# A hybrid decoder layer on one core: the second up projection with wide products, and its weight sums made in DRAM by GpSimd

## The chip, the core and the metric

The kernel runs on one core of one Trainium2 chip. The metric is the device time of one execution in microseconds (us); the median of three executions stands for a kernel. A core has five engines with one instruction queue each, worked off in order: PE (TensorE, matrix products, with PEld for loading the stationary operand), DVE (VectorE), ACT (ScalarE), POOL (GpSimd) and SP (SyncE, which here only issues transfers). Transfers run on 16 DMA engines that all issuing engines share.

## The reference

One layer of a decoder over 512 tokens of width 1024, in float32:

```python
x = x + 0.5 * swiglu(rmsnorm(x, ffn1_norm), ffn1_wg, ffn1_wu, ffn1_wd)
x = x + hybrid_mixer(rmsnorm(x, mix_norm), w_in, ...)     # attention and recurrence, 64 small products
x = x + 0.5 * swiglu(rmsnorm(x, ffn2_norm), ffn2_wg, ffn2_wu, ffn2_wd)
out = rmsnorm(x, final_norm)

def swiglu(x, w_gate, w_up, w_down):                      # 1024 -> 2816 -> 1024
    return (silu(x @ w_gate) * (x @ w_up)) @ w_down
```

## The kernel before

**Precision.** The products take a rounded float32 type. A weight tile `wr` is split by `wsplit` into a rounded part `wh` (a copy on ACT) and the remainder `wl` (a subtraction on DVE), and an activation likewise into two parts, so a float32 product becomes three matmuls: high by high, high by remainder and remainder by high.

**Stages, in order of time.** First up projection (a direct part, then a block part), first down projection, the mixer (`run_jobs`, 64 jobs named by `ORDER`; most have 24 matmuls of 512 columns, the eight `A` jobs have 12), second up projection, second down projection. Both up projections are the function `ffn_up`, both down projections `block_down`.

**`ffn_up`.** Eight direct products come first (`direct`). The other weights are taken in 2 by 2 blocks, with seven block products in place of eight: 18 groups `w` in the second up projection, and so 126 products in the list `stream`, each named by a number `p` from 1 to 7 and a group. A product has four k-steps of 128. Its moving operands (`moving_operands`) are tiles `cm` whose left 256 columns (`lo`) are the rounded part and whose right 256 (`hi`) the remainder. The seven products need sums of weight blocks, s1 to s4. `load` brings the blocks of a group into SBUF (SP), adds two of them to others in flight (transfers by POOL with an addition), and `add_weights` makes the last two sums on DVE. `prepare` splits the weights of the product four ahead (`LEAD`). `results` takes a finished product out of PSUM: ACT copies, DVE adds or multiplies, ACT applies silu.

**The mixer's order.** `run_jobs` is written out by a planner: `Plan` keeps a clock for each engine, and `due` issues the next step of a chain when the plan says that its inputs are there. `mixer_begin` (at the second k-step of a job) copies the high part of the weights of the job two later, `mixer_prepare` (at the fourth) makes the remainder. `gate_weights` loads the small gate weights `wrg` of the eight recurrent jobs x0 to x7, three jobs ahead (`AHEAD`), by POOL into a tile `gr`, which ACT then copies to `gw`. Between the jobs the weight sums of the second down projection are made in DRAM (`Blocks`, `sums_in_turn`): the first two transfers of a block by SP, the other six by POOL; of a kernel's 64 such transfers 16 stand in SP's queue and 48 in POOL's.

**Buffers.** Raw weights `wr` have three buffers (`RAWS`), the split parts `wh` and `wl` three each, a PSUM tag (`mm`, `aux`) four banks each.

Of the kernel before, what the change touches and what calls it, by code (L numbers as in the profile page):

```python
# [9 lines left out]
F32 = mybir.dt.float32  # L10
# [33 lines left out]
LEAD = 4  # L44
PLAIN, PAIRS, TAIL = 6, 8, 3
DIRECT = 4
SUMJOBS = 48


ORDER = """  # L50
# [125 lines left out]
def hybrid_kernel(ctx, tc, xt, vec, w1u, w1d, wm, wki, wrg, watt, wrnn, wout, w2u, w2d, gf, out):  # L176
# [139 lines left out]
    class Blocks:  # L316
# [6 lines left out]
        def stages(self):  # L323
            plain, adds = nc.gpsimd.dma_start, lambda o, i: nc.gpsimd.dma_start(o, i, accum_op=ALU.add)  # L324
            return [
                [(nc.sync.dma_start, self.s1, self.a21), (nc.sync.dma_start, self.s3, self.a21)],
                [(adds, self.s1, self.a22), (adds, self.s3, self.a11)],
                [(plain, self.s2, self.s1)],
                [(adds, self.s2, self.a11)],
                [(plain, self.s4, self.s2)],  # L330
                [(adds, self.s4, self.a12)],
            ]

    def sums_in_turn(blocks):

        lists, groups = [b.stages() for b in blocks], []
        for n in range(len(lists) + 5):
            groups.append([t for u in range(max(0, n - 5), min(n + 1, len(lists))) for t in lists[u][n - u]])
        return groups

    def moving_operands(g):

# [56 lines left out]
        V.tensor_mul(tu, tu, tg)  # L399
        return tu  # L400

    def ffn_up(y, wu, n0, hs, g, waiting=(), given=(), ahead=None):

# [6 lines left out]
        H = KD // 2 * P  # L410
        f0 = n0 + DIRECT
        count = KF - f0
        ws = []

        direct = [(n, j) for n in range(n0, f0) for j in range(2)]
        raws, split_, sums, gates = list(given), [], [], []

        def fetch():
            if len(raws) < len(direct):
                r = raw.tile([P, WMAX], F32, tag="raw", name=nm("wr"))  # L420
                Q.dma_start(r, wu[direct[len(raws)]])
                raws.append(r)

        def prepare_direct():
# [30 lines left out]
        class W:  # L455
            pass

        def load(w):

# [31 lines left out]
                V.tensor_add(o.s4, o.s2, o.x[:, H:])  # L491

        def prepare(i):
            if i < LEAD:
                add_weights(i)
            if i + 1 >= LEAD:
                add_weights(i + 1)
            p, w = stream[i]
            o = ws[w]
            if i % 2 == 0:  # L500
                units.append([wsp.tile([P, WMAX], F32R, tag=t, name=nm(t)) for t in ("wh", "wl")])
            h, l = (t[:, i % 2 * H:(i % 2 + 1) * H] for t in units[i // 2])
            wsplit({1: lambda: o.x[:, :H], 2: lambda: o.x[:, H:], 6: lambda: o.s2, 5: lambda: o.s1, 7: lambda: o.s3,
                    4: lambda: o.a22, 3: lambda: o.s4}[p](), h, l)

        def products(i):
            p, w = stream[i]
            o = ws[w]
            if p == 1:
                o.beta = psum("mm")  # L510
            elif p == 2:
                o.p2 = psum("aux")
            elif p == 5:
                o.gamma = psum("aux")
            acc_ = {2: lambda: o.p2, 5: lambda: o.gamma, 3: lambda: o.gamma}.get(p, lambda: o.beta)()[:, lo]
            h, l = (t[:, i % 2 * H:(i % 2 + 1) * H] for t in units[i // 2])
            starts, opens = p in (1, 2, 5), dict(skip_group_check=p not in (1, 2, 5))
            for j in range(KD // 2):
                c = slice(j * P, (j + 1) * P)
                m = moving[{1: "n11", 2: "b21", 6: "t2", 5: "t1", 7: "r", 4: "q", 3: "n22"}[p]][j]  # L520
                T.matmul(acc_, h[:, c], m[:, lo], start=starts and j == 0, stop=False, **opens)
                T.matmul(acc_, h[:, c], m[:, hi], start=False, stop=False, **opens)
                T.matmul(acc_, l[:, c], m[:, lo], start=False, stop=j == KD // 2 - 1, **opens)

        def results(i):
            p, w = stream[i]
# [30 lines left out]
        with tc.manual_schedule(engines=ENGINES):  # L557
# [4 lines left out]
            for d, (n, j) in enumerate(direct):  # L562
# [13 lines left out]
                if d == 0:  # L576
                    for _ in range(3):
                        next(norm)
                if d in (4, 6):
                    load_ = load(len(ws))  # L580
                if d >= 4:
                    next(load_, None)
                if d > 1:
                    next(operands, None)
# [4 lines left out]
                pass  # L589
            for i in range(len(stream)):  # L590
                products(i)
                if i:
                    results(i - 1)
                else:
                    together(results_direct(len(direct) - 1))
                if i + LEAD < len(stream):
                    prepare(i + LEAD)
                elif not ahead or i + LEAD - len(stream) < PLAIN - f0:
                    halve(hs, f0 + i + LEAD - len(stream))
                if ahead:  # L600
                    ahead(i - len(stream))
                if i % 14 == 12 and i // 14 < f0:
                    halve(hs, i // 14)
                if i % 7 == 1 and len(ws) < count:
                    load_ = load(len(ws))
                next(load_, None)
            results(len(stream) - 1)

    def halve(hs, n):

# [252 lines left out]
    d1 = block_down(hs, w1d, sums)  # L863
    ffn_up(y, w1u, 2, hs, V_G1, ((WP[0], WP[1]), (WP[2], pu)), AH[1:], d1.tasks_at)

    BLOCKS2D = down_blocks(w2d)
    cc = const.tile([P, 8], F32, name="cc")
    hb = vt[:, V_BX:V_BX + 8]

# [401 lines left out]

    idles = []
    lasts, starts_ = {}, {}
    sum_groups, sums_done = sums_in_turn(BLOCKS2D), [0]

    def run_jobs():
        ws = mixer_ws
# [2 lines left out]
        for i, job in enumerate(jobs):  # L1280
# [6 lines left out]
            for k in range(n):  # L1287
# [10 lines left out]
                if k == 2:  # L1298
                    due_sums = len(sum_groups) * (i + 1) // SUMJOBS
                    while sums_done[0] < min(due_sums, len(sum_groups)):  # L1300
                        for move, o, s_ in sum_groups[sums_done[0]]:
                            move(o, s_)
                        sums_done[0] += 1
                if k == 3:
                    mixer_prepare()
                    mixer_fetch()
                if k == n - 1:
# [456 lines left out]
        then(lastD + m - 1, norm_second, m, 1)  # L1764
        then(lastD + m + 1, scaled, m)

    ffn_up(y2, w2u, 0, hs, V_G2, ahead=tasks_at)
# [88 lines left out]
```

## Time and profile before

| what | value |
|---|---|
| median of three executions | 1070.22 us (1070.16 to 1070.58) |
| the profiled execution | 1070.87 us, span 1068.9 us |
| first up projection, block part (78 to 238 us) | PE busy 160.00 of 160 us, DVE 122.38, ACT 92.40 |
| mixer (350 to 728 us) | PE busy 377.63 of 378 us, DVE 314.00, ACT 251.88, POOL 37.80 |
| second up projection, block part (768.5 to 950 us) | PE busy 181.50 of 181.5 us, DVE 137.66, ACT 103.84, POOL 29.83 |
| second down projection (950 us to the end) | PE busy 112.01 of 118.9 us, DVE 88.69, ACT 67.80 |

The span runs from the first to the last instruction of the profiled execution; some 2 us lie around it. Busy shares are of a stage's time. Nearly every instruction has line L170, a helper that records all operations for the planner, so the groups are told apart by the names of their tiles: `wl<-wr,wh` is the remainder of a raw weight, `mm<-cm,wh` a product of a moving operand with a high part.

### The profile page before, as it was taken

What the parts mean: (1) busy time and instruction counts of PE and PEld (TensorE: products, weight loads), DVE (VectorE), ACT (ScalarE), POOL (GpSimd) and SP (SyncE); (2) the same over time, 40 slices, a digit from 0 to 9 for tenths busy, and PEclk for the clock granted to TensorE, in tenths of its full rate; (3) what the DMA queues carried; (4) which work ended last, traced back from release to release, by engine and by line L of the source; (5) the groups of instructions that cost most, each with busy time, mean ns of one, the idle gap of its engine ahead of it and who ended that gap; (6) DMA issues with size and microseconds to landing.
All of it is one profiled execution on the core that took longest, in us unless ns stands there. A gap on an engine that the chain in (4) does not pass through costs nothing.

```text
span 1068.9 us, 17652 instructions
## 1 busy us (share of the span) xinstructions
PE 1058.7 (99%) x6412; PEld 947.6 (89%) x6412; DVE 847.3 (79%) x1614; ACT 658.6 (62%) x1279; POOL 168.2 (16%) x210
## 2 busy tenths in 40 slices
PE   9999999999999999999999999999999999999997
PEld 7889999999989888888888888888899999998886
DVE  6687777779979779999899867766877777779865
ACT  6565655556466657976886664446656555565663
POOL 0161111102341011212120000001511111100020
PEclk9999999999999999999999999999999999999999
DMA  7297767638994486676593211434977776635583
GB/s 277 70 256 192 171 181 203 158 107 238 236 236 118 120 235 165 178 194 181 121 223 107 79 50 50 138 105 112 250 193 165 185 195 170 158 101 175 178 207 128
DMA packets 81718, 176.48 MB, mean 165 GB/s; under 512 B 9824, under 2 KB 18144, under 8 KB 81376
## 3 DMA queue, kind: packets, MB, share of 16 engines
q1 hardware_dynamic: 54672, 129.95, 37.2%
q0 software_dynamic: 26240, 44.58, 24.7%
q8 instruction: 50, 0.82, 0.3%
q10 hardware_dynamic: 720, 0.84, 0.2%
q14 instruction: 36, 0.29, 0.1%
HBM read 164.32 MB, written 18.87 MB: 171 GB/s over the span
## 4 chain that ended last, share of the span: by engine, by line
PE 91%; DMA 3%; DVE 2%; ACT 2%; issue 1%; SPq 0%; ACTq 0%; POOLq 0%
PE mm L170 64%; PE aux L170 27%; DMA sm<-w1d 1%; DMA a<-w1d 1%; DVE wl L170 1%; DMA wr<-w1u 1%; ACT wh L170 1%; DMA cm<-cb 1%; DVE ca L170 0%; ACT cm L170 0%; ACT L170 0%; DVE cm L170 0%; DVE h L170 0%; ACT rl L170 0%; DVE cb L170 0%
## 5 line engine op out<-in xcount | busy, mean ns | idle before, releaser
L170 DVE TENSOR_TENSOR wl<-wr,wh 128x512 fp32r<-128x512 f32 (+2 forms) x226 | 205.7, 914 | 86.3 <-ACT wh L170 85.7
L170 PE MATMUL mm<-cm,wh 128*128 128x256 f32 x1472 | 268.7, 283 | 0.6 <-ACT wh L170 0.5
L170 PEld LDWEIGHTS mm<-cm,wh 128*128 128x128 f32 x1472 | 230.1, 192 | 1.6 <-ACT wh L170 1.0
L170 ACT ACTIVATE wh<-wr 128x512 fp32r<-128x512 f32 (+3 forms) x228 | 181.5, 802 | 65.3 <-issue 23.0
L170 PE MATMUL mm<-cm,wl 128*128 128x256 f32 x736 | 208.5, 283 | 0.4 <-DVE wl L170 0.4
L170 PE MATMUL mm<-yh,wh 128*128 128x512 f32 (+1 forms) x416 | 164.1, 395 | 0.5 <-ACT wh L170 0.3
L170 PE MATMUL mm<-yl,wh 128*128 128x512 f32 (+1 forms) x416 | 162.3, 391 | 0.0
L170 PE MATMUL aux<-cm,wh 128*128 128x256 f32 x880 | 161.8, 283 | 0.5 <-DMA cm<-cb 0.5
L170 PE MATMUL mm<-yh,wl 128*128 128x512 f32 x408 | 159.1, 390 | 0.0
L170 PEld LDWEIGHTS mm<-cm,wl 128*128 128x128 f32 x736 | 141.3, 192 | 0.9 <-DVE wl L170 0.9
L170 PEld LDWEIGHTS aux<-cm,wh 128*128 128x128 f32 x880 | 137.3, 192 | 0.7 <-DMA cm<-cb 0.7
L170 PE MATMUL aux<-cm,wl 128*128 128x256 f32 x440 | 124.5, 283 | 0.0
L170 DVE TENSOR_TENSOR wl<-s,wh 128x512 fp32r<-128x512 f32 x144 | 98.6, 687 | 24.5 <-ACT wh L170 22.7
L170 ACT ACTIVATE wh<-s 128x512 fp32r<-128x512 f32 x144 | 87.6, 622 | 38.9 <-DVE s L170 30.9
L170 PEld LDWEIGHTS mm<-yh,wh 128*128 128x128 f32 (+1 forms) x416 | 78.1, 188 | 17.4 <-ACT wh L170 0.6
L170 PEld LDWEIGHTS mm<-yl,wh 128*128 128x128 f32 (+1 forms) x416 | 77.7, 187 | 15.6 <-DVE yl L170 0.3
L170 PEld LDWEIGHTS mm<-yh,wl 128*128 128x128 f32 x408 | 76.7, 188 | 16.4
L170 PEld LDWEIGHTS aux<-cm,wl 128*128 128x128 f32 x440 | 84.5, 192 | 0.0
L170 PE MATMUL mm<-wh,cm 128*128 128x512 f32 x192 | 59.0, 389 | 0.0
L170 ACT ACTIVATE tg<-mm 128x256 f32<-128x256 f32 x68 | 26.1, 383 | 52.9 <-PE mm L170 52.7
L324 POOL DMA_DIRECT2D scr<-w2d x32 | 30.1, 1011 | 176.3 <-DMA scr<-w2d 162.0
L158 POOL DMA_DIRECT2D s<-w2u x36 | 33.5, 1077 | 126.9 <-DMA s<-w2u 100.9
(244 smaller groups left out, 1987.6 us busy)
## 6 DMA issues: line engine op xcount, KB each, us to landing
wr<-wm SPq DMA_DIRECT2D x39, 512.0 KB, 4.4
wr<-w2u SPq DMA_DIRECT2D x26, 512.0 KB, 5.3
wr<-w1u SPq DMA_DIRECT2D x21, 512.0 KB, 5.3
wr<-w1d SPq DMA_DIRECT2D x18, 512.0 KB, 4.1
s<-w2u SPq DMA_DIRECT2D x36, 256.0 KB, 5.9
s<-w2u POOLq DMA_DIRECT2D x36, 256.0 KB, 5.1
wr<-w2d SPq DMA_DIRECT2D x36, 256.0 KB, 3.0
s<-w1u SPq DMA_DIRECT2D x32, 256.0 KB, 5.8
```

The costliest lines, as they stand in the source:

```text
L158: return self.engine.dma_start(out, src, **kw)
L170: return call(*args, **kw)
L324: plain, adds = nc.gpsimd.dma_start, lambda o, i: nc.gpsimd.dma_start(o, i, accum_op=ALU.add)
```

## The change

Three things change, all in or for the second up projection.

1. **Wide products.** In the block part of the second up projection a k-step's two matmuls of the high part (by `lo`, then by `hi`, both added into the left half of a bank) become one of 512 columns into the whole bank; the matmul of the remainder stays 256 wide. The two halves of a bank have to be added afterwards: `wide_step`, with `copies` and `reads`, takes the place of `results`.
2. **Weight sums in DRAM.** The sums of the 18 groups are made in DRAM like those of the second down projection, all by POOL, and read like plain weights: a pair of products takes two transfers of 256 KB by SP into one raw tile, split in one instruction each on ACT and DVE. `load` and `add_weights` are not used there any more. There are now 26 blocks of 8 transfers, 208 in all; 162 are issued in the mixer's jobs 7 to 60 and 46 in the block part. Ahead of each batch POOL copies one column of a weight tile made at that time (`beat`), which holds the batch back till then.
3. **Gate weights.** The loads of `wrg` go from POOL's queue to ACT's, and are begun eight jobs ahead; the planner adds 12 us to the time at which it thinks them there.

```diff
-AHEAD = 3
+AHEAD, GATELAG = 8, 12.0
-SUMJOBS = 48
+SUMS_FROM, SUMS_TO, SUMS_PART = 7, 60, 0.78
     # Blocks.stages
-                [(nc.sync.dma_start, self.s1, self.a21), (nc.sync.dma_start, self.s3, self.a21)],
+                [(plain, self.s1, self.a21), (plain, self.s3, self.a21)],
     # products
+            for j, m in enumerate(ms if blocks else ()):
+                T.matmul(both, h[:, j * P:(j + 1) * P], m, start=starts and j == 0, stop=False, **opens)
+            for j, m in enumerate(ms):
                 c = slice(j * P, (j + 1) * P)
-                T.matmul(acc_, h[:, c], m[:, lo], start=starts and j == 0, stop=False, **opens)
-                T.matmul(acc_, h[:, c], m[:, hi], start=False, stop=False, **opens)
+                if not blocks:
+                    T.matmul(acc_, h[:, c], m[:, lo], start=starts and j == 0, stop=False, **opens)
+                    T.matmul(acc_, h[:, c], m[:, hi], start=False, stop=False, **opens)
                 T.matmul(acc_, l[:, c], m[:, lo], start=False, stop=j == KD // 2 - 1, **opens)
     # prepare, for a pair of products
+            if blocks:
+                if i % 2 == 0:
+                    units.append([wsp.tile([P, WMAX], F32R, tag=t, name=nm(t)) for t in ("wh", "wl")])
+                    wsplit(raws[len(direct) + i // 2], *units[-1])
+                    fetch()
+                return
     # the results of a wide product, two of four kinds
+            if p == 2:
+                V.tensor_sub(o.c, o.p2, o.c)
+                joined(o.t1[:, lo], o.c)
+            elif p == 3:
+                V.tensor_add(o.e, o.gamma, o.e)
+                V.scalar_tensor_tensor(o.t1[:, hi], o.e[:, lo], -1.0, o.e[:, hi], op0=ALU.mult, op1=ALU.subtract)
     # the sums' transfers
+    def sums_until(part, after):
+        if sums_done[0] < part * len(sum_moves):
+            nc.gpsimd.tensor_copy(beat, f(after[:, :1]))
+        while sums_done[0] < part * len(sum_moves):
+            move, o, s_ = sum_moves[sums_done[0]]
+            move(o, s_)
+            sums_done[0] += 1
     # gate_weights
-        G.dma_start(r, wrg[t])
+        nc.scalar.dma_start(r, wrg[t])
+        plan.copy(r, wrg[t], "POOL")
+        plan.ready[r.name] += GATELAG
```

On PE, one product of kind 2 in the block part of the second up projection (`aux` is its PSUM bank, `cm` the moving operand of a k-step, `wh` and `wl` the two parts of its weights). Before:

```order
L170 MATMUL aux_8709<-cm_8117,wh_8618 128x256 x2
L170 MATMUL aux_8709<-cm_8117,wl_8619 128x256
L170 MATMUL aux_8709<-cm_8203,wh_8618 128x256 x2
L170 MATMUL aux_8709<-cm_8203,wl_8619 128x256
L170 MATMUL aux_8709<-cm_8303,wh_8618 128x256 x2
L170 MATMUL aux_8709<-cm_8303,wl_8619 128x256
L170 MATMUL aux_8709<-cm_8391,wh_8618 128x256 x2
L170 MATMUL aux_8709<-cm_8391,wl_8619 128x256
```

The same product in the changed kernel:

```order
L170 MATMUL aux_8922<-cm_8481,wh_8844 128x512
L170 MATMUL aux_8922<-cm_8574,wh_8844 128x512
L170 MATMUL aux_8922<-cm_8655,wh_8844 128x512
L170 MATMUL aux_8922<-cm_8395,wl_8845 128x256
L170 MATMUL aux_8922<-cm_8481,wl_8845 128x256
L170 MATMUL aux_8922<-cm_8574,wl_8845 128x256
L170 MATMUL aux_8922<-cm_8655,wl_8845 128x256
```

With the wide matmul of `cm_8395` just ahead of these rows, twelve matmuls of 256 columns have become four of 512 and four of 256, the wide ones first.

On ACT, the gate weights of a recurrent job late in the mixer. Before, the load stands in POOL's queue, and ACT has only the copy `gw<-gr`, between the copies of weights `wh` of two jobs:

```order
L170 ACTIVATE wh_5591<-wr_5437 128x1024
L170 ACTIVATE QS_5626<-mm_5583 64x512
L170 ACTIVATE QS_5627<-mm_5583 64x512
L170 ACTIVATE gw_5635<-gr_5634 128x256
L170 ACTIVATE wh_5641<-wr_5489 128x1024
```

In the changed kernel the load of `gr` stands in ACT's own queue, and the copy that needs it is the next instruction:

```order
L170 ACTIVATE wh_5410<-wr_5205 128x1024
L170 ACTIVATE rl_5417<-aux_5370 128x512
L170 ACTIVATE rl_5434<-aux_5381 128x512
L170 ACTIVATE sg_5448<-mm_5403 128x512
L1177 DMA gr_5454<-wrg 128x256
L170 ACTIVATE gw_5455<-gr_5454 128x256
L170 ACTIVATE wh_5461<-wr_5263 128x1024
```

This is job x5. The loads for x0, x1, x6 and x7 stand in the same way directly ahead of their copy; for x2, x3 and x4 other ACT work lies between.

On POOL, a stretch of the mixer in the changed kernel (`scr` is a sum's tile in DRAM, L324 a transfer that adds, L985 a plain one):

```order
L982 COPY beat<-wh_5410 128x1
L985 DMA scr_2962<-scr_2961 16x4096
L324 DMA scr_2969<-w2u 128x512
L982 COPY beat<-wl_5411 128x1
L324 DMA scr_2971<-w2u 128x512
L982 COPY beat<-wh_5461 128x1
L985 DMA scr_2977<-w2u 128x512
L985 DMA scr_2979<-w2u 128x512
```

Before, POOL's transfers in the mixer were the 48 sums and the eight loads of `wrg`, with no copy between; now two reads of weight tiles a job stand between them, and the loads of `wrg` are gone from this queue.

More of the change, by code (lines that the diff above doesn't have):

```diff
@@ L334, in sums_in_turn @@
     def sums_in_turn(blocks):
[L336 to L339, printed above, removed]
+        lists = [b.stages() for b in blocks]
+        return [t for n in range(len(lists) + 10) for u, l in enumerate(lists)
+                if 0 <= n - u <= 10 and (n - u) % 2 == 0 for t in l[(n - u) // 2]]
     def moving_operands(g):
@@ L400, in ffn_act, with weight_blocks, ffn_up @@
         return tu
-    def ffn_up(y, wu, n0, hs, g, waiting=(), given=(), ahead=None):
+    def weight_blocks(wu, n0):
+        H = KD // 2 * P
+        got = []
+        for w in range(KF - n0 - DIRECT):
+            u, v = (wu[n0 + DIRECT + w // 2 * 2 + i, w % 2] for i in range(2))
+            got.append(Blocks(u[:, :H], u[:, H:], v[:, :H], v[:, H:]))
+        return got
+    class W:
+        pass
+    def ffn_up(y, wu, n0, hs, g, waiting=(), given=(), ahead=None, blocks=None):
         H = KD // 2 * P
@@ L412, in ffn_up, with source @@
         count = KF - f0
-        ws = []
+        ws = [W() for _ in range(count)] if blocks else []
+        for w, o in enumerate(ws):
+            o.j = w % 2
         direct = [(n, j) for n in range(n0, f0) for j in range(2)]
         raws, split_, sums, gates = list(given), [], [], []
+        def source(i):
+            p, w = stream[i]
+            b = blocks[w]
+            return {1: b.a11, 2: b.a12, 3: b.s4, 4: b.a22, 5: b.s1, 6: b.s2, 7: b.s3}[p]
         def fetch():
-            if len(raws) < len(direct):
+            n = len(raws)
+            if n < len(direct):
                 r = raw.tile([P, WMAX], F32, tag="raw", name=nm("wr"))
-                Q.dma_start(r, wu[direct[len(raws)]])
+                Q.dma_start(r, wu[direct[n]])
+                raws.append(r)
+            elif blocks and 2 * (n - len(direct)) < len(stream):
+                r = raw.tile([P, WMAX], F32, tag="raw", name=nm("wr"))
+                for i in range(2):
+                    Q.dma_start(r[:, i * H:(i + 1) * H], source(2 * (n - len(direct)) + i))
                 raws.append(r)
@@ new lines, in wide_step @@
+        def wide_step(i):
+            ready = functions[:]
+            functions.clear()
+            done = stream[i - 1] if i else None
+            if done:
+                p, o, first = done[0], ws[done[1]], ws[done[1] - 1]
+                copies(p, o)
+                if p in (2, 3):
+                    reads(p, o, first)
+            if i + LEAD < len(stream):
+                prepare(i + LEAD)
+            if done and p not in (2, 3):
+                reads(p, o, first)
+            for t in ready:
+                A.activation(t, t, AF.Silu)
@@ L578, in ffn_up @@
                         next(norm)
-                if d in (4, 6):
+                if blocks:
+                    pass
+                elif d in (4, 6):
                     load_ = load(len(ws))
-                if d >= 4:
+                if d >= 4 and not blocks:
                     next(load_, None)
@@ L603, in ffn_up @@
                     halve(hs, i // 14)
+                if blocks:
+                    if i % 2 == 0:
+                        sums_until(SUMS_PART + (1 - SUMS_PART) * min(1.0, i / (0.9 * len(stream))), units[-1][1])
+                    continue
                 if i % 7 == 1 and len(ws) < count:
@@ L606, in ffn_up @@
                 next(load_, None)
-            results(len(stream) - 1)
+            if blocks:
+                wide_step(len(stream))
+            else:
+                results(len(stream) - 1)
     def halve(hs, n):
@@ L1306, in run_jobs @@
                     mixer_fetch()
+                if k in (1, 3) and mixer_begun:
+                    step = (i + (k - 1) / 4 - SUMS_FROM) / (SUMS_TO - SUMS_FROM)
+                    sums_until(SUMS_PART * min(step, 1.0), mixer_begun[-1][k == 3 and 2 or 1])
                 if k == n - 1:
@@ L1765, in hybrid_kernel @@
         then(lastD + m + 1, scaled, m)
-    ffn_up(y2, w2u, 0, hs, V_G2, ahead=tasks_at)
+    ffn_up(y2, w2u, 0, hs, V_G2, ahead=tasks_at, blocks=BLOCKS2U)
     with tc.manual_schedule(engines=ENGINES):
```

66 lines of the change are left out of this document (50 added, 16 removed).

## The prediction

> **What bounds the kernel now.** I read the page first: the span, the engines' shares and the chain that ended last.
>
> ```profile
> span 1068.9 us, 17652 instructions
> PE 1058.7 (99%) x6412; PEld 947.6 (89%) x6412; DVE 847.3 (79%) x1614; ACT 658.6 (62%) x1279; POOL 168.2 (16%) x210
> PE 91%; DMA 3%; DVE 2%; ACT 2%; issue 1%; SPq 0%; ACTq 0%; POOLq 0%
> ```
>
> PE is busy in 1058.7 of 1068.9 us, and 91% of the chain is PE. So time is gained only where PE gets fewer or shorter matmuls, and lost wherever PE is made to wait. Next the windows, by stage.
>
> ```profile
> 350.00:425.00 75.00, 75.00 (x347) 61.07 (x346) 63.28 (x109) 48.88 (x81) 10.10 (x14) 1.00 0.63 171
> 425.00:450.00 25.00, 24.84 (x110) 20.21 (x109) 23.32 (x36) 24.77 (x36) 5.52 (x8) 1.00 0.62 165
> 450.00:475.00 25.00, 25.00 (x116) 20.84 (x115) 24.19 (x49) 20.21 (x33) 4.96 (x7) 1.00 0.79 205
> ...
> 750.00:775.00 25.00, 25.00 (x140) 21.88 (x139) 21.93 (x42) 17.18 (x42) 15.04 (x17) 1.00 1.13 252
> 775.00:800.00 25.00, 25.00 (x210) 25.00 (x210) 18.52 (x34) 14.40 (x31) 3.51 (x4) 1.00 0.75 190
> ```
>
> The columns are the stretch, then the busy time of PE, PEld, DVE, ACT and POOL, the granted clock, the DMA share (above 1 where packets overlap) and GB/s. Two things are to be seen. PE has no gap in the mixer (the first three rows) or in the second up projection, but from 425 to 450 us ACT is busy for 24.77 of 25 us: there any new wait on ACT has nowhere to go. In the block part (last row) DVE and ACT have room. How long a matmul takes is read from the starts in the timeline of PE, since the busy times of neighbours overlap.
>
> ```profile
> 768.00 0.40 PE L170 MATMUL mm<-cm,wh 128*128 128x256 f32 x2
> 768.24 0.28 PE L170 MATMUL mm<-cm,wl 128*128 128x256 f32 x1
> 768.36 0.40 PE L170 MATMUL mm<-cm,wh 128*128 128x256 f32 x2
> ...
> 949.32 0.28 PE L170 MATMUL aux<-cm,wl 128*128 128x256 f32 x1
> 949.44 1.04 PE L170 MATMUL mm<-ident,x 128*128 128x128 f32 x8
> ```
>
> ```profile
> 690.00 0.39 PE L170 MATMUL mm<-mh,wh 128*128 128x512 f32 x1
> 690.23 0.39 PE L170 MATMUL mm<-ml,wh 128*128 128x512 f32 x1
> 690.46 0.39 PE L170 MATMUL mm<-mh,wl 128*128 128x512 f32 x1
> 690.68 0.39 PE L170 MATMUL mm<-mh,wh 128*128 128x512 f32 x1
> ```
>
> The block part runs from 768.00 to 949.44: 181.44 us for 126 products of 12 matmuls, 0.120 us each, without a gap. A matmul of 512 columns starts 0.227 us after the one before it (0.68 for three).
>
> **The change part by part: PE.** A product had 12 matmuls of 256: 1.440 us. Now it has 4 of 512 and 4 of 256: 4 x 0.227 + 4 x 0.120 = 1.387 us. That saves 0.053 us a product and 126 x 0.053 = 6.7 us in all. No row shows a narrow matmul behind a wide one, so its pitch is bounded: 256 more columns cost 0.227 - 0.120 = 0.107, which would be all if the 0.013 fixed part vanished, and 0.133 if it doubled. The saving then lies between 13.4 and 0 us. I take 0.120, the row of the same matmul.
>
> PEld is busy throughout the block part, so the 0.120 might also be the pace of loading weights; with two loads in 0.347 us that would be no limit any more. The Trainium skill (TensorE: Matmul & The Clock Gate, Wait — 56ns, not 53.3ns?) gives warm matmuls N / 2.4 GHz plus about 2.5 ns from start to start. By that a removed matmul saves 2.5 ns, 504 x 2.5 = 1.3 us. The rows disagree: 0.227 and 0.120 leave 13 ns over their columns, and the sum goes by them.
>
> **DVE and ACT in the block part.** Before and after are compared by groups, per two groups of weights (14 products).
>
> ```profile
> L170 DVE TENSOR_TENSOR wl<-wr,wh 128x1024 fp32r<-128x1024 f32 x102 | 124.5, 1221 | 37.4 <-ACT wh L170 37.0
> L170 DVE TENSOR_TENSOR wl<-s,wh 128x512 fp32r<-128x512 f32 x144 | 98.6, 687 | 24.5 <-ACT wh L170 22.7
> L170 DVE TENSOR_TENSOR s<-s,wr 128x512 f32<-128x512 f32 x68 | 46.5, 683 | 0.0
> L170 DVE TENSOR_TENSOR tg<-aux,tg 128x256 f32<-128x256 f32 x34 | 14.2, 418 | 0.7 <-ACT tg L170 0.7
> ```
>
> DVE loses four sums (4 x 0.683 = 2.7 us), and 14 splits of 0.687 become 7 of 1.221 (9.6 to 8.5). Its results grow: two adds of 512 and their joinings at kinds 2 and 7, an add at kind 4, an add and a subtraction at kind 3. At 0.42 for 256 columns and 0.69 for 512 that is 4.1 before and 9.1 after. So 16.4 becomes 17.6 us, while PE's 14 products shrink from 20.2 to 19.4. DVE's measured 18.52 of 25 (74%) scales to 83%. ACT reads PSUM 512 wide but splits in fewer instructions; by the same counting it goes from 58% to about 63%. Both stay hidden behind PE; were DVE the bound, its added 1.2 us would cost 9 x 1.2 = 11 us.
>
> **Raw weights in the block part.** A pair of products takes 2.77 us and one raw tile of 512 KB, in two transfers. With three tiles, a tile's turn must fit into 3 x 2.77 = 8.3 us: two issues of 0.325, the landing, ACT's split 1.06 and DVE's 1.22. That leaves 5.4 us for the landing.
>
> ```profile
> L158 SPq DMA_DIRECT2D wr<-scr x32: 319/325/1110, 980.4 to 1031.5; - x32
> L170 ACT ACTIVATE wh<-wr 128x1024 fp32r<-128x1024 f32 x102 | 107.6, 1055 | 40.5 <-issue 15.7 <-PE aux L170 9.5 <-PE mm L170 7.1
> wr<-scr SPq DMA_DIRECT2D x32, 256.0 KB, 3.1
> a<-w2u SPq DMA_DIRECT2D x18, 256.0 KB, 6.1
> ```
>
> The nearest rows are the same transfers in the second down projection, 3.1 us, and the last of four issued together in the block part of before, 6.1. The changed block part has two at a time and fewer additions in flight (46 POOL transfers where there were 36 into SBUF and four loads a group), so I take 4.5: no cost.
>
> **Sums in the mixer.** From 450 to 565 us the DMA view shows what the sums use now.
>
> ```profile
> q0 software_dynamic: 3438, 8.74, 40.1%
> scr<-w2d POOLq DMA_DIRECT2D x20, 256.0 KB, 6.5
> scr<-scr POOLq DMA_DIRECT2D x10, 256.0 KB, 8.5
> gr<-wrg POOLq DMA_DIRECT2D x1, 128.0 KB, 5.9
> ```
>
> POOL's queue took 40.1% of 115 us for 31 transfers, 1.49 us of all engines each. 162 of them are 241 us, in 53 of 64 jobs, about 313 us: a share of 0.77. The loads of weights alone took 27.3% (600 to 725 us):
>
> ```profile
> q1 hardware_dynamic: 3456, 10.49, 27.3%
> wr<-wout SPq DMA_DIRECT2D x8, 512.0 KB, 3.5
> ...
> wr<-wm SPq DMA_DIRECT2D x39, 512.0 KB, 4.4
> ```
>
> Together 1.04, below the 1.13 at which PE ran without a gap from 750 to 775 us. A late weight load has three jobs of 5.4 us less 2.3 for its splits to land, against 3.5 alone and 4.4 over the whole mixer: I cost it at nothing; were that cover gone, each microsecond of lateness would be one of PE's.
>
> **Gate weights on ACT.** This is the term I fear. For five of the eight jobs the copy `gw` stands right behind the load in ACT's queue, so ACT, which works in order, stands still for the whole landing; queued behind are the weight split of a job two later and the emptying of PSUM. The bounds for a landing of 128 KB:
>
> ```profile
> wr<-w1u ACTq DMA_DIRECT2D x2, 128.0 KB, 4.0
> ...
> DMA to landing us min/median/max: 2.3/5.4/7.0
> ```
>
> The first row is the only one on ACT's queue, the second that of `gr` on POOL's. I take 4.0. The Trainium skill (DMA: Bandwidth & Descriptors, Anatomy of one DMA) fits 2.0 us plus bytes over 436 GB/s, an estimate of 2.3 us here, which is the row's minimum; by it the term below would vanish. The loads of x0 and x1 fall where ACT has room (48.88 of 75). Those of x5, x6 and x7 fall between some 430 and 470 us.
>
> ```profile
> 457.82 1.28 ACT L170 ACT_TABLE_LOAD   x1
> ...
> 464.47 1.06 ACT L170 ACTIVATE wh<-wr 128x1024 fp32r<-128x1024 f32 x1
> ...
> 472.68 0.60 ACT L170 ACTIVATE gu<-mm 128x512 f32<-128x512 f32 x1 [3.83 <-PE mm L170]
> 467.43 1.22 DVE L170 TENSOR_TENSOR wl<-wr,wh 128x1024 fp32r<-128x1024 f32 x1
> ```
>
> Three landings are 12.0 us. The new order has two ACT table loads less, 2.6 us, so ACT would be 9.4 us late at 464. The remainder of the job that starts when PE ends `mm` at about 472.6 is ready at 468.65 on DVE: 4.0 us of lead. What is left, 5.4 us, PE waits; behind it ACT's own idle 3.83 us takes the rest. With landings of 2.3 us the wait is 0.3, with 7.0 it is 14.4. The 4.0 is from the kernel's start, where all first loads are in flight at once, so I take the middle between its 5.4 and the 0.3, about **3.0 us**.
>
> **Sum.** 1070.87 - 6.7 + 3.0 = 1067.2 for an execution like the profiled one, which lies 0.65 above the median: **1066.5 us**, 0.35% faster. A measurement of this kernel tells about 0.2%, 2.1 us, from no change.
>
> **Rivals.**
>
> 1. *No change.* The same wait on ACT at the 4.0 row or a little above costs 5 to 8 us and eats the gain: 1069 to 1072, say 1070. ACT's 24.77 of 25 speaks for it; against it that other transfers leave ACT's ring to `gr` alone. 0.24.
> 2. *Slower: the raw tiles pace the block part.* It decides from a landing of 5.4 us. At the 6.1 of before a tile's turn is 9.0 us, 3.01 a pair instead of 2.77: 63 x 0.24 = 15 us, less the 2.7 us that the first splits are ahead: 12. So 1066.5 + 12 = 1078.5. For it speak the 5.5 to 6.1 us of today's block part, against it the 3.1 of the down projection with its loads as dense. 0.12.
> 3. *Slower: POOL's read holds a weight tile.* DVE may not write a `wl` again before POOL has read it, three jobs later. In the eight short jobs of the mixer (12 matmuls, 2.72 us) POOL has three transfers a job.
>
> ```profile
> L324 POOL DMA_DIRECT2D scr<-w2d x32: 797/858/1635, 376.2 to 562.9; - x32
> ```
>
> At the median that is 2.6 us and just fits; at the 1.635 maximum POOL is 8 x 2.2 = 18 us late, 8.2 more than three short jobs allow: about 10 us, 1076. It decides from some 1.2 us a transfer. 0.08.
>
> 4. *The fixed part stays.* If the narrow matmul rose to 0.131 behind wide ones, near its bound, 1.0 us would be saved and 3.0 lost: 1072.2. The measured 0.227 and 0.120 speak against it. 0.04. By the 2.5 ns of the Trainium skill's page on TensorE, named above, the saving would be 1.3 us.
>
> **How the numbers follow.** My forecast has 0.52, from 1062 to 1068. Faster by over 0.2%: 0.52. Within 0.2%: rivals 1 and 4, 0.28. Slower: 2 and 3, 0.20. The range of 1062 to 1074 leaves out the lower end of PE's bounds and most of rivals 2 and 3.
>
> **What would show it.** In the changed profile: eight matmuls a product and some 175 us for the block part (right), or a pitch above 1.40 us with waits for `wr` (rival 2); ACT idle of about 3 to 4 us ahead of five `gw<-gr`, and PE gaps in the mixer between 440 and 490 us that sum to 3 us; DVE near 83% in the block part; no wait of DVE or ACT for POOL. I am wrong if PE's gaps lie elsewhere, if the mixer has none (then about 1063.5), or if the narrow matmuls keep another pitch.

## The result, and the profile after

| kernel | median of its runs | ratio to before, 95% interval |
|---|---|---|
| before | 1070.40 us (1070.16 to 1071.85) | |
| changed | 1083.37 us (1080.80 to 1090.39) | 1.0129 [1.0081, 1.0177] |

The change makes the kernel slower by 1.3%. 1066.5 us was forecast, with a range up to 1074. The profiled execution took 1083.15 us. Its page and its chain:

```profile
span 1081.4 us, 17187 instructions
PE 1059.4 (98%) x5908; PEld 921.0 (85%) x5908; DVE 862.0 (80%) x1587; ACT 665.5 (62%) x1232; POOL 286.9 (27%) x477
PE 75%; DMA 10%; ACT 7%; DVE 6%; issue 2%; SPq 0%; ACTq 0%; POOL 0%; DVEq 0%; POOLq 0%
```

504 matmuls are gone, but the chain that was 91% PE is now 75% PE, 10% DMA, 7% ACT and 6% DVE: PE has to wait. Where, the windows show (columns as before):

```profile
425.00:450.00 25.00, 24.85 (x110) 20.26 (x109) 22.93 (x37) 24.31 (x35) 10.87 (x19) 1.00 0.71 183
450.00:475.00 25.00, 19.95 (x88) 15.36 (x87) 16.33 (x23) 18.65 (x29) 10.60 (x18) 1.00 0.78 198
...
675.00:700.00 25.00, 23.30 (x94) 18.53 (x94) 17.41 (x24) 9.47 (x13) 17.09 (x32) 0.93 1.07 318
...
800.00:825.00 25.00, 25.00 (x145) 21.86 (x144) 22.40 (x35) 15.87 (x23) 6.14 (x14) 1.00 0.81 246
...
925.00:950.00 25.00, 24.08 (x135) 20.72 (x135) 20.73 (x31) 13.95 (x22) 5.37 (x12) 1.00 0.91 242
950.00:975.00 25.00, 21.28 (x119) 17.73 (x118) 19.06 (x34) 16.23 (x38) 0.00 (x0) 1.00 0.42 143
```

There are three places: 5.05 us idle from 450 to 475, 1.7 from 675 to 700 with the clock at 0.93, and 4.6 from 925 to 975. The waits of PE name what ended each:

```profile
PE mm L170 <- ACT e L170: 3.7, 2, 2.8
PE mm L170 <- DVE xl L170: 2.3, 1, 2.3
PE mm L170 <- ACT i L170: 1.7, 1, 1.7
...
PE mm L170 <- ACT mh L170: 1.1, 1, 1.1
```

The columns are the sum in us, the number of waits and the longest. The largest name results (`e`, `xl`, `i`, `mh`), not weights: PE waits for work of ACT and DVE that was queued behind something late. The ledger below follows one and the same matmul in PE's timeline of both kernels: its start in the changed kernel less its start before (354.21, 657.36, 768.00, 950.23 and 1061.62 us, the last matmul), and so what each stage adds. It is made from each kernel's profiled execution; e3's is 4.7 us above its median, e1's 2.0 below. The A jobs are the mixer's eight short ones, the O jobs its last eight.

| us lost (+) or won (-) | to the mixer's norm | mixer to the A jobs | A and O jobs, direct part | block part | down projection | sum | median of runs |
|---|---|---|---|---|---|---|---|
| changed | -0.9 | +6.6 | +4.2 | +1.3 | +1.1 | +12.3 | 1083.4 |
| forecast | 0 | +3.0 | 0 | -6.7 | 0 | -3.7 | 1066.5 |
| e8 gates alone | -0.7 | +7.0 | +0.3 | 0.0 | +0.1 | +6.7 | 1077.2 |
| e1 copies late | -0.7 | +3.8 | +2.2 | +3.1 | 0.0 | +8.3 | 1082.0 |
| e9 gates as before | -1.5 | +21.9 | +4.6 | +3.4 | +0.1 | +28.5 | 1099.0 |
| e2 sums even | -0.7 | +8.1 | +1.2 | +3.5 | +0.1 | +12.2 | 1083.9 |
| e7 four raw tiles | +3.2 | +9.5 | -0.1 | -3.7 | +0.7 | +9.6 | 1079.7 |
| e3 last pair first | -0.1 | +6.6 | +4.2 | +2.1 | +0.8 | +13.6 | 1079.7 |
| e5 no down sums | -0.7 | +6.7 | +2.4 | -4.3 | +1.1 | +5.2 | 1074.5 |
| e6 narrow | -0.8 | +7.1 | +2.8 | +7.2 | 0.0 | +16.4 | 1086.9 |
| e4 wide alone | +0.2 | 0.0 | 0.0 | +2.2 | +3.3 | +5.8 | 1076.1 |
| e10 sums in the direct part | +0.2 | +30.0 | +1.1 | +9.6 | +1.1 | +41.9 | 1111.9 |
| e11 the same, narrow | +0.5 | +28.2 | +1.0 | +12.4 | 0.0 | +42.1 | 1113.2 |
| e12 all apart | -0.7 | +5.1 | +2.8 | -3.5 | +1.1 | +4.7 | 1074.1 |
| e13 the same, narrow | -0.5 | +4.5 | +2.2 | +0.3 | 0.0 | +6.5 | 1078.3 |
| e14 block sums kept | -0.1 | +0.4 | +1.3 | -0.3 | +0.8 | +2.0 | 1074.1 |
| e15 no sums in A jobs | -0.3 | +0.4 | +0.1 | -3.8 | +0.7 | -2.8 | 1068.3 |
| e16 none in the block part | +0.5 | +0.5 | +8.1 | -4.4 | +0.8 | +5.5 | 1075.2 |

### The profile page after: what moved, and what is told of

Its sections match the earlier page's. It is cut to its first block, busy times and chain, and to the rows that moved or that the text cites. A ratio compares the mean times of both kernels' runs of the same rounds, so it can differ in the third digit from the quotient of the medians.

```text
span 1081.4 us, 17187 instructions
## 1 busy us (share of the span) xinstructions
PE 1059.4 (98%) x5908; PEld 921.0 (85%) x5908; DVE 862.0 (80%) x1587; ACT 665.5 (62%) x1232; POOL 286.9 (27%) x477
## 4 chain that ended last, share of the span: by engine, by line
PE 75%; DMA 10%; ACT 7%; DVE 6%; issue 2%; SPq 0%; ACTq 0%; POOL 0%; DVEq 0%; POOLq 0%
PE mm L170 51%; PE aux L170 23%; DVE wl L170 3%; ACT wh L170 3%; DMA wr<-w2u 2%; DMA gr<-wrg 1%; DMA sm<-w1d 1%; DMA wr<-scr 1%; ACT L170 1%; DMA s<-w1d 1%; DMA wr<-w1u 1%; DMA wr<-wout 1%; DMA wr<-watt 1%; ACT r L170 1%; DMA cm<-cb 1%
## 5 line engine op out<-in xcount | busy, mean ns | idle before, releaser
L170 DVE TENSOR_TENSOR wl<-wr,wh 128x1024 fp32r<-128x1024 f32 (+2 forms) x253 | 258.0, 1023 | 101.0 <-ACT wh L170 94.1
L170 ACT ACTIVATE wh<-wr 128x1024 fp32r<-128x1024 f32 (+3 forms) x255 | 225.6, 890 | 104.9 <-issue 24.3
L170 PE MATMUL mm<-cm,wh 128*128 128x256 f32 (+1 forms) x1184 | 242.6, 311 | 4.1 <-ACT e L170 3.7
L170 PEld LDWEIGHTS mm<-cm,wh 128*128 128x128 f32 x1184 | 189.4, 191 | 12.8 <-ACT e L170 4.3
L170 PE MATMUL mm<-cm,wl 128*128 128x256 f32 x736 | 172.7, 282 | 0.2 <-DVE wl L170 0.2
L170 PE MATMUL aux<-cm,wh 128*128 128x256 f32 (+1 forms) x664 | 141.6, 320 | 0.3 <-DMA cm<-cb 0.3
L170 PEld LDWEIGHTS aux<-cm,wh 128*128 128x128 f32 x664 | 106.8, 191 | 5.4 <-DMA cm<-cb 0.5
L324 POOL DMA_DIRECT2D scr<-w2u x72 | 62.7, 902 | 8.6 <-issue 6.2
L170 DVE TENSOR_TENSOR wl<-s,wh 128x512 fp32r<-128x512 f32 x72 | 49.2, 687 | 11.8 <-ACT wh L170 11.0
L982 POOL COPY beat<-wh 128x1 f32<-128x1 f32 x53 | 31.3, 591 | 102.7 <-ACT wh L170 102.4
```

What stands on the lines that cost most here:

```text
L170: return call(*args, **kw)
L982: nc.gpsimd.tensor_copy(beat, f(after[:, :1]))
```

## The experiments

**The gate weights (e8, e1, e9).** First their part of the change alone, in the kernel before:

```diff
-AHEAD = 3
+AHEAD, GATELAG = 8, 12.0
-        G.dma_start(r, wrg[t])
+        nc.scalar.dma_start(r, wrg[t])
+        plan.copy(r, wrg[t], "POOL")
+        plan.ready[r.name] += GATELAG
```

> The kernel before with the change of the gate weights alone: loads in ACT's queue, begun eight jobs ahead, no further sums. Theory A (the price is the landing on a queue by itself, 4.0 us as at the kernel's start): PE waits 3 us between 450 and 480 us, 1073.5. Theory A2 (the landing is 6.4 us also without the added sums): 6.3 us as in the changed kernel, 1076.5. Rival B (only the load of the added sums makes the wait): landings of 2.3 to 3 us, no wait, 1070.

Measured: 1077.24 us, 1.0059 [1.0044, 1.0074]: theory A2. The rows of ACT in this run, a load and then its copy, with the idle time ahead of it in brackets:

```profile
452.45 0.34 ACTq L1055 DMA_DIRECT2D gr<-wrg  x1
457.33 0.42 ACT L170 ACTIVATE gw<-gr 128x256 fp32r<-128x256 f32 x1 [3.28 <-DMA gr<-wrg]
470.86 0.34 ACTq L1055 DMA_DIRECT2D gr<-wrg  x1
477.49 0.42 ACT L170 ACTIVATE gw<-gr 128x256 fp32r<-128x256 f32 x1 [4.85 <-DMA gr<-wrg]
```

These are the loads of x6 and x7. They land 4.9 and 6.6 us after their issue, and ACT stands still for most of that. This needs neither the added sums nor the wide products. In e1 (changed kernel) the load is really ahead of its copy:

```diff
-        plan.copy(r, wrg[t], "POOL")
-        plan.ready[r.name] += GATELAG
+        plan.writer[r.name] = "DMA"
+        plan.ready[r.name] = plan.time["PE"] + GATELAG
```

> The changed kernel with one edit: the planner takes a gate weight as landed 12 us after PE's planned time instead of 12 us after its POOL clock, so that 12 to 18 other ACT instructions stand between each load of x5, x6 and x7 and its copy. Theory A (each loss stands by itself): PE's lateness of 6.3 us between 453 and 478 us goes, the other losses stay, 1083.4 - 6.3 = about 1077. Rival B (the losses share one cause, the transfers' load, and move on when one place is relieved): PE loses the same 4 to 6 us at another place of the mixer, 1081 to 1083. The new order has four table loads more on ACT (5 us of ACT's time), which by A lie in ACT's idle time.

Measured: 1082.03 us, 1.0108 [1.0092, 1.0125]. No instruction waits for `gr` any more, and PE has no gap between 440 and 480 us. But 3.6 us come at 430 us, where the planner's other order has ACT busy for over 4.9 of each 5 us (29 table loads instead of 25): PE waits 2.23 us for ACT's `i`, and the clock is at 0.73 from 430 to 435 us. And the block part loses 1.8 more. Neither theory was right as a whole: the cause is confirmed, its cure was not free. e9 goes the other way, to the loads of before (the two removed lines of the first diff, in the changed kernel):

> The changed kernel with the gate weights as before (POOL's queue, three jobs ahead, the planner as before), so that ACT's and DVE's order in the mixer is that of before; POOL's queue now holds the sums and their reads as well. Theory A (the gates' part costs its 6.6 us here as it does by itself): PE has no gap from 440 to 480 us, the gap and clock drop at 690 us (2 to 4 us) and the block part's waits stay: 1077. Rival B (behind the held-back sums the gate weights land late): ACT waits for gr by some us at two or three jobs, 1080 or more.

Measured: 1099.01 us, 1.0265 [1.0251, 1.0279]. ACT's and POOL's waits in the mixer of e9:

```profile
POOL beat L982 <- ACT wh L170: 125.7, 40, 7.1
POOL beat L982 <- DVE wl L170: 79.0, 17, 56.3
ACT gw L170 <- DMA gr<-wrg: 29.1, 5, 8.3
```

Rival B, and far worse than it said. Before, POOL waited in the mixer for its own transfers, 15 to 19 us at a time, but for no fresh weight tile. Its queue ran ahead of the program all the same: the last load of `gr` was issued at 465.4 us for a copy at 496.9. With the reads of `beat` in it, POOL is held to the time of the program, the load comes when ACT is about to need it, and ACT waits up to 8.3 us. So the sums forced the gate weights out of POOL's queue, and ACT's queue, which is in order with the copy, gives a load no lead either where it stands directly ahead of its copy.

**The A jobs (e2).** The sums are dealt out by matmuls:

```diff
-                    step = (i + (k - 1) / 4 - SUMS_FROM) / (SUMS_TO - SUMS_FROM)
+                    step = (sum(columns(j)[0] for j in jobs[SUMS_FROM:i]) + k) / STEPS if i >= SUMS_FROM else 0.0
```

> The changed kernel with one edit: the 162 sums of the mixer are dealt out by matmuls instead of by jobs, so that a short A job (12 matmuls) gets 1.7 transfers and not 3.06, and a long one 3.3. Theory A: the landings of wr<-watt and wr<-wout between 660 and 690 us fall from 6.6 to 8.1 to about 4 us, PE has no gap at 690 us, the clock stays at 1.00, and 3.9 us go: about 1079.5. Rival B (any sums beside those loads make them late): gap and clock drop stay, 1083. The rest of the mixer gets 8% more transfers per us; if that costs, it shows before 650 us.

Measured: 1083.88 us, 1.0121 [1.0106, 1.0136]. At the A and O jobs PE loses what theory A said, 1.2 us instead of 4.2, with one gap of 0.58 and the clock at 1.00. But the loads of `wout` still land after 7.0 us there (theory A: some 4); ACT stands for weights for 2.8 us from 660 to 700 us, in the changed kernel for 8.7, in e15 not at all. The total is rival B's: the mixer before them loses 1.5 more and the block part 2.2 more. What the transfers do from 650 to 700 us, in the changed kernel and then in e15 (650 to 690 us; none of its sums is issued from 657.7 to 681.3; last column: median us from issue to landing):

```profile
scr<-w2d POOLq DMA_DIRECT2D x16, 256.0 KB, 10.3
wr<-wout SPq DMA_DIRECT2D x7, 512.0 KB, 7.5
```

```profile
wr<-wout SPq DMA_DIRECT2D x7, 512.0 KB, 3.5
scr<-w2d POOLq DMA_DIRECT2D x4, 256.0 KB, 5.0
```

**The block part (e5, e7, e3, e6).** e5 makes no sums for the down projection (`sums_in_turn(BLOCKS2U)`, `SUMS_PART = 1.0`), so none are made beside the block part.

> The changed kernel without the 64 transfers that make the sums of the second down projection, which reads plain blocks in their place (a part of the computation is left out); the other 144 are dealt out in the mixer, 2.7 a job instead of 3.06, and none stands beside the block part. Theory A (the additions beside the block part make the raw tiles land in 5.7 to 7.2 us): landings there fall to 4 us, no wait for wr of over 1 us, PE has no gap, the block part takes 126 x 1.405 = 177 us instead of 182.7, about 1077.5. Rival B (the ring of three raw tiles and the order of SP's queue set the pace): the gaps of 3 to 4 us stay, 1082.

Measured: 1074.53 us, 1.0039 [1.0026, 1.0051]. Theory A: the block part wins 4.3 us (and the A and O jobs, at 2.7 sums a job, lose 1.8 less). e7 gives the ring of raw tiles a fourth one:

```diff
-    raw = ctx.enter_context(tc.tile_pool(name="raw", bufs=RAWS))
+    raw = ctx.enter_context(tc.tile_pool(name="raw", bufs=4))
-SLOTS = 60
+SLOTS = 58
```

> The changed kernel with four raw weight tiles instead of three (and 58 slots instead of 60, for the room; the planner's order in the mixer shifts a little by that). Theory A (a raw tile's turn is too short): a turn has 11.2 us in the block part and a job more in the mixer, so the block's gaps go (182.7 to 177) and the gap and clock drop at 690 us shrink by more than half; only the 6.3 us of the gate weights stay: 1074 to 1076. Rival B (the DMA engines are full, a share of 0.88 in the block part and 1.07 in the A jobs, so a tile that is asked for earlier only waits longer): landings grow by as much, 1081 or more.

Measured: 1079.69 us, 1.0081 [1.0066, 1.0096]. The weights' landings in the late block part (870 to 950 or 960 us) of the changed kernel, of e5 and of e7:

```profile
wr<-scr SPq DMA_DIRECT2D x31, 256.0 KB, 4.7
wr<-w2u SPq DMA_DIRECT2D x22, 256.0 KB, 4.5
```

```profile
wr<-scr SPq DMA_DIRECT2D x29, 256.0 KB, 2.8
wr<-w2u SPq DMA_DIRECT2D x21, 256.0 KB, 3.0
```

```profile
wr<-scr SPq DMA_DIRECT2D x30, 256.0 KB, 5.3
wr<-w2u SPq DMA_DIRECT2D x22, 256.0 KB, 5.6
```

Both theories of e7 saw half. A tile asked for earlier does land later (5.3 and 5.6 us), and still the block part wins 3.7 and the A and O jobs lose nothing, since the longer turn covers it. What e7 wins there it gives back in part before the mixer (+3.2) and in it (+9.5 instead of 6.6). e3 changes one order, the last pair ahead of the down projection's first:

```diff
+            if blocks:
+                fetch()
             for i in range(len(stream)):
                 products(i)
```

> The changed kernel with one edit: one pair of weights more is fetched before the block part, so the last pair of the second up projection is loaded ahead of the first pair of the down projection, and takes its raw tile ahead of it. Theory A (the 2.8 us wait of PE near 954 us is the order of these two loads in the ring of raw tiles): the 2.8 us go, 1080.6, and the down projection's first pair has room. Rival B (the ring as such is too slow in the last third of the block part: landings of 5.7 to 7.2 us against a turn that leaves 5.4): the wait moves a pair on or into the first products of the down projection, 1083.

Measured: 1079.72 us, 1.0093 [1.0071, 1.0115]. Three of its four runs are 3 to 4 us below the changed kernel's median, as theory A has it; the profiled one was the fourth (1084.41), and in it the wait of 2.8 us at the end is 0.4, with others of 1.7 and 1.1 ahead of it. The intervals of the two kernels overlap, and the profiled run's block part loses 2.1 us, not less than the changed kernel's 1.3. So the wait at the end comes from the order, but it isn't the block part's whole loss, and what the order is worth is not shown.

e6 puts the narrow products back into the changed kernel (the loops of `products`, `results` for `wide_step`).

> The changed kernel with the narrow products of before: sums in DRAM, gate weights and mixer as changed, twelve matmuls of 256 columns a product. Theory A (raw tiles pace the block part): PE needs 126 x 0.035 = 4.4 us more, but a turn of three pairs has 8.64 us instead of 8.43, so most of the block's 4 to 5 us of gaps go: the same time as changed, 1082 to 1084, and the wide products bring nothing where they stand. Rival B (the gaps come from the wide results on ACT and DVE, 512 columns instead of 256): no gap at all in the block part, 181.4 us there. If the wide products are worth their 4.4 us in spite of all: 1087.

Measured: 1086.90 us, 1.0150 [1.0135, 1.0166]. Its third case, 1087. The narrow products wait as the wide ones do (7.2 us lost in the block part), so the wide results aren't the cause, and the wide products keep their saving, 3.5 us between the medians.

**The wide products alone (e4).** In the kernel before, with `wide_step` and the wide matmuls, `load` and `add_weights` as they were:

> The kernel before with the wide products alone: sums in SBUF on DVE, gate weights on POOL and the mixer as before. By the pitches of the changed kernel (0.232 us for 512 columns, 0.119 for 256) PE needs 1.405 us a product, 126 x (1.440 - 1.405) = 4.4 us less, and by the prediction's 0.227 and 0.120 6.7 us less. Theory A (DVE becomes the bound without the sums in DRAM: some 20.0 us of DVE for 14 products against 19.7 us of PE): DVE busy 97% or more in the block part, most of the saving lost, 1068 to 1070. Rival B (DVE keeps up): 1066 with the pitch 0.232, 1063.7 with 0.227.

Measured: 1076.06 us, 1.0045 [1.0030, 1.0060]. Theory A, and dearer than it said. DVE in e4, two windows of the block part, then what PE waited for:

```profile
830.00:890.00 60.00, 57.84 (x328) 50.04 (x327) 57.77 (x105) 36.90 (x74) 10.55 (x12) 1.00 0.71 176
890.00:949.00 59.00, 57.99 (x331) 50.09 (x329) 55.95 (x101) 36.60 (x73) 7.01 (x8) 1.00 0.61 155
```

```profile
PE mm L170 <- ACT c L170: 3.8, 7, 0.9
PE aux L170 <- DVE e L170: 1.8, 1, 1.8
```

DVE is busy 57.77 of 60 us. Counted to the same number of matmuls (here two products of the block part stand behind the down projection's first matmul), PE loses 2.2 us in the block part, where it wins 4.4 in e16, and 3.3 more in the first products of the down projection. Without the sums in DRAM the wide products are a loss.

**Several causes at once (e10 to e16).** e10 is e9 with the sums dealt out over jobs 4 to 63 and, by one line in `ffn_up`, the direct part, and none beside the block part; e11 the same with narrow products.

```diff
                 if blocks:
-                    pass
+                    sums_until(SUMS_PART + (1 - SUMS_PART) * (d + 1) / len(direct), split_[-1][1])
```

> The kernel of the run before this one, with the 208 sums dealt out by matmuls over jobs 4 to 63 (87%, 3.2 a long job, 1.6 a short one) and over the direct part of the second up projection (13%), and none beside the block part. Theory A (what is left of the loss is where transfers are too dense: the short A jobs and the block part): no gap at 690 us, none in the block part, 126 x 1.405 = 177 us there, some 1 us at the start of the down projection: 1070.6 - 4.4 + 1 = 1067, faster than both kernels. Rival B (any 208 transfers cost PE somewhere, 64 of them did not): 1071 to 1075.

> The same with the narrow products of before. Theory A (a wide product saves 0.035 us where nothing else waits): 4.4 us more than the run before this one, block part 181.4 us without a gap, 1070.5 to 1071.5. Rival B (the saving is the predicted 0.053): 6.7 us more. Rival C (wide results on DVE and ACT cost at the block part's end what the products save): less than 2 us more.

Measured: 1111.91 us, 1.0384 [1.0370, 1.0399], and 1113.23 us, 1.0399 [1.0385, 1.0413]. No theory held. The mixer has e9's waits, and the block part of e10 begins with one of 8.70 us of PE for `cm`: the block part's moving operands are transfers of POOL too, and now stood behind the sums. From 850 to 950 us, without a sum beside it, e10's block part has no gap (PE busy in 100.00 of 100 us). The pair says little about the wide products, since both wait.

e12 keeps ACT's queue with e1's two lines and `GATELAG` 9, and deals out all 208 sums over jobs 4 to 63; e13 is e12 with narrow products; e14 is e1, e2 and e3 together with `GATELAG` 9.

> The changed kernel with two edits: the planner holds each gate weight's copy back by 9 us of PE's planned time (7 or more ACT instructions stand between load and copy), and all 208 sums are dealt out by matmuls over jobs 4 to 63, 3.7 a long job and 1.9 a short one, none beside the block part. Theory A (the gates, the dense sums in the A jobs and the sums beside the block part are the whole loss): mixer within 2 us of before, block part 177 us, 1 us at the start of the down projection, 1067 to 1069, faster than before. Rival B (any order with the gate weights on ACT costs 3 us or more, since ACT is full there): 1070 to 1073. Rival C (3.7 sums a job are too many): waits for wr all over the mixer, 1075 or more.

> The same with the narrow products of before. If a wide product saves 0.035 us where nothing waits: 4.4 us less the 1 us that the wide results cost at the start of the down projection, so 3.4 us slower than the run before this one. If the predicted 0.053 held: 6.7 slower. If the wide results cost as much as they bring: within 1 us.

> The changed kernel with the gate weights' copy held back by 9 us, the 162 sums of the mixer dealt out by matmuls, and the last pair fetched ahead of the down projection's first; the 46 sums beside the block part stay. Theory A: mixer as in the run with all apart, block part 178 to 180 us (waits of 1 to 3 us for wr stay, the one at its end goes), 1069 to 1072, 2 to 3 us slower than that run. Rival B (the wait at the block part's end is the whole of its loss): as fast as that run.

Measured: e12 1074.12 us, 1.0032 [1.0020, 1.0043]; e13 1078.30 us, 1.0072 [1.0059, 1.0085]; e14 1074.13 us, 1.0048 [1.0030, 1.0067]. e14 came out 2 us slower than its theory A: the block part still loses some 4 us to its sums (5.7 in the changed kernel, 7.5 and 7.9 in e1 and e2, each against the 4.4 that e16 wins), and 1.3 stay at the A and O jobs. It shows that gate weights on ACT need cost nothing (mixer +0.4), against e12's rival B. e12 lost 5.1 us in the mixer at one place, first in ACT's timeline, then in PE's:

```profile
399.91 1.06 ACT L170 ACTIVATE wh<-wr 128x1024 fp32r<-128x1024 f32 x1 [4.25 <-DMA wr<-wm]
```

```profile
401.43 0.39 PE L170 MATMUL aux<-KI,QI 128*128 128x256 f32 x1 [3.21 <-ACT rl L170]
```

The weight load is issued at 394.71 us, in e14 at 389.03: in SP's queue it stands behind copies of the index queries (`QI`), and one of these is issued at 390.94 us instead of 384.85. Sums run beside them in e12, from job 4 on, and not in e14, from job 7; what held that copy was not tried by itself. e13 is 4.2 us slower than e12 by the medians, 2.7 by the profiles' block and down parts: the wide products are worth about the expected 3.4.

e15 and e16 are e14 with the sums dealt out over jobs 7 to 63 without the eight A jobs; e15 keeps 25 of them beside the block part, e16 none:

```diff
-                if k in (1, 3) and mixer_begun:
-                    step = (i + (k - 1) / 4 - SUMS_FROM) / (SUMS_TO - SUMS_FROM)
+                if k in (1, 3) and i >= SUMS_FROM and job[0] != "A":
+                    step = (sum(shares(j) for j in jobs[SUMS_FROM:i]) + k) / STEPS
```

> The changed kernel with the gate weights' copy held back by 9 us, the sums dealt out by matmuls over jobs 7 to 63 without the eight A jobs (88%, 3.7 a job), the other 25 beside the block part, and the last pair fetched first. Theory A (the causes are complete): the mixer within 0.5 us of before, the block part 178 to 179 us, 1 us at the start of the down projection: 1068 to 1069, faster than both. Rival B (a loss is left that follows the number of transfers, not their place): the mixer loses 2 us or more somewhere, 1071 to 1074.

> The same with all 208 sums in those jobs, 4.2 a job, and none beside the block part. Theory A: the block part 177.5 us or less; the mixer as in the run before this one if 4.2 sums a job still leave the weights in time, 1067 to 1068.5. Rival C (4.2 is too dense): waits for wr in the mixer of 2 us or more, which eat the gain, 1070 or more.

Measured: e15 **1068.30 us, 0.9978 [0.9969, 0.9987]**, faster than both kernels, than the one before by 0.2%; e16 1075.18 us, 1.0045 [1.0031, 1.0059]. In e15 theory A holds in every stage. Its chain in the block part, 24 matmuls (three products) in 4.21 us without a break:

```profile
843.58 2.81 PE mm L170 x16
846.39 1.40 PE aux L170 x8
```

e16 is rival C, but not by waits for `wr`. The chain of e16 before the second norm:

```profile
712.18 10.45 DMA scr<-w2d
...
723.15 6.29 DMA scr<-scr
...
730.53 0.20 POOL beat L984
...
730.76 0.04 DVE wl L170
...
731.90 0.70 DVE acc L170
```

POOL, late by two transfers of 10.45 and 6.29 us, reads a weight tile late; DVE may not write that tile's next `wl` before, and `acc`, which PE waits for 6.2 us, stands behind it. This is the mechanism of the forecast's third rival. In the changed kernel no engine waits for `beat`.

## Why the prediction was wrong

Three waits that the forecast put at 3.0 us, nothing and nothing took 6.6, 4.2 and 5.7; the saving itself came out as 4.4 instead of 6.7. The columns of the ledger's first two rows are the forecast's steps.

1. **"Gate weights on ACT": right mechanism, 3.0 us forecast, 6.6 measured** (6.7 to 7.0 by itself, e8). The changed kernel, ACT and then PE:

```profile
451.41 0.34 ACTq L1177 DMA_DIRECT2D gr<-wrg  x1
458.17 0.42 ACT L170 ACTIVATE gw<-gr 128x256 fp32r<-128x256 f32 x1 [5.17 <-DMA gr<-wrg]
```

```profile
465.98 0.50 PE L170 MATMUL mm<-xl,gw 128*128 128x512 f32 x1 [2.28 <-DVE xl L170]
471.87 0.50 PE L170 MATMUL mm<-yh,wh 128*128 128x512 f32 x1 [1.70 <-ACT i L170]
```

   The landings of x5, x6 and x7 were as long together as forecast (2.0, 6.7 and 3.9 us, for three of 4.0), but one of them, x6's, cost most of it: ACT stands still for 5.17 us of it, and PE waits 5.0 us between 459 and 472 us (the two rows, with 0.48 and 0.58 ahead of them). So the 4.0 us of lead weren't there. They were read from the next job's weights, while PE came to wait for the recurrent job's own `xl` and for a bank that ACT frees by `i`. The 5.4 before it was halved would have been nearer; the price is that of rival 1. The fit that the forecast took here from the Trainium skill (DMA: Bandwidth & Descriptors, Anatomy of one DMA) is one of transfers issued by GpSimd, and these stood on ACT's queue: its 2.3 us is near the fastest of the eight loads, 2.0, and far from x6's 6.7.

2. **"Sums in the mixer ... I cost it at nothing": 4.2 us.** The mean share over the mixer was the wrong measure, and "three jobs of 5.4 us" the wrong cover: an A job lasts 2.72, so three are 8.2, and 3.06 sums fall into each. The share there is 1.07, below the 1.13 that the forecast took for harmless, and yet `wout` lands after 7.5 us instead of 3.5, and PE loses 1.7 by waits, 1.6 more by the clock and the rest in short delays beside them. With no sums in the A jobs (e15) 0.1 us is left of the 4.2; with fewer of them there (e14) it is 1.3.

3. **"So I take 4.5: no cost": 5.7 us** (1.3 lost where 4.4 are to be won, e5 and e16). The median was right, 4.7 and 4.5 us, but single landings reach 5.7 to 7.3, and a ring of three with a limit of 5.4 falls behind on the long ones and can't catch up, since PE takes a pair every 2.81 us; with a fourth tile (e7) the block part wins 3.7, though its landings are longer. The wait doesn't show as one for weights: ACT stands for `wr`, and the copies `c` and `e`, which PE needs before it may add to their bank again, stand behind it. The chain of the largest wait, 2.79 us:

```profile
948.66 4.25 DMA wr<-scr
...
953.01 1.06 ACT wh L170
954.07 0.49 ACT e L170
...
954.61 1.67 PE mm L170 x8
```

   This load is the last pair's; it is issued late, behind the down projection's first at 945.37, and that order is what e3 changes. The step is rival 2 at half its price.

4. **The saving on PE: 4.4 us, not 6.7.** The narrow matmul was right (0.47 us for four in the rows below, 0.118 each; forecast 0.120, rival 4 is out), the wide one has 0.232 where 0.227 was read in the mixer: (0.232 - 0.227) x 504 = 2.5 us. In the changed kernel:

```profile
778.86 0.64 PE L170 MATMUL mm<-cm,wl 128*128 128x256 f32 x4
779.33 1.09 PE L170 MATMUL aux<-cm,wh 128*128 128x512 f32 x4
780.26 0.63 PE L170 MATMUL aux<-cm,wl 128*128 128x256 f32 x4
```

   Four wide ones take 0.93. By the Trainium skill's 2.5 ns beside the columns (TensorE: Matmul & The Clock Gate, Wait — 56ns, not 53.3ns?) the saving would have been 1.3 us, an estimate; e5 and e16 won 4.3 and 4.4. The same pitch stands in e15's block part (2.81 us for 16 matmuls), where PE hardly waits (busy in 178.19 of 178.4 us), so waits don't make it; why it is not 0.227 stays open.

5. **DVE and ACT hidden: right inside the block part, not at its end.** DVE is busy in 54.03 of 65 us from 860 to 925 us, the forecast 83% (in the window shown, 22.40 of 25), and PE waits for none of it there. But the last wide results are still with DVE when the down projection starts, 0.7 to 1.1 us in nine of the kernels with wide products (3.3 in e4, up to 0.1 in e1, e2 and e9, which stays open) and up to 0.1 with narrow ones. The forecast had no term for it.

From the ledger's first row the profiled time is 1070.9 - 0.9 + 6.6 + 4.2 + 1.3 + 1.1 = 1083.2; by the ledger's making that must agree with the 1083.15 measured. What carries the causes are the experiments.

## What to carry to other kernels

A transfer that stands just ahead of its reader in the program is early only on a queue that may run ahead of the program; put a wait into that queue, or move the transfer to the reader's own, and most of its landing may be paid (5.2 of 6.7 us at x6). Count added transfers per stage of like pace, not as a mean, and compare a ring of buffers with the longest landing there. An experiment that spares one cause may move work into another queue's way (e9, e10): look for what else lives on it.

## What was not expected of the hardware

After some short waits the granted clock falls for about 3 us. PE of the changed kernel after waits of 1.12 and 0.58 us:

```profile
691.30 0.49 PE L170 MATMUL mm<-mh,wh 128*128 128x512 f32 x1 [1.12 <-ACT mh L170]
692.38 0.50 PE L170 MATMUL mm<-ml,wh 128*128 128x512 f32 x1 [0.58 <-DVE ml L170]
...
694.17 0.63 PE L170 MATMUL mm<-ml,wh 128*128 128x512 f32 x1
694.60 0.63 PE L170 MATMUL mm<-mh,wl 128*128 128x512 f32 x1
695.02 0.63 PE L170 MATMUL mm<-mh,wh 128*128 128x512 f32 x1
...
697.06 0.39 PE L170 MATMUL mm<-mh,wl 128*128 128x512 f32 x1
```

From 693.7 to 696.7 us a matmul of 512 columns takes 0.427 us, not 0.227: eight of them cost 1.6 us, as much again as the waits. The Trainium skill (TensorE: Matmul & The Clock Gate, What's actually happening) gives half the clock after an idle window of some 3.4 us, and its section Wait — 56ns, not 53.3ns? 426.7 ns for 512 columns at it. The pitch agrees to the digit; the condition doesn't, since less than 2 us of waiting did it here, and a single wait of 2.23 us in e1 (at 432 us) and of 2.02 in e8 (at 465 us), while waits of 2.28 and 1.70 us between 463 and 472 us of the changed kernel did not. What decides it stays open.
